# Log-softmax backward: the second y as one 64 KiB-run load, the first group's exp through PSUM, the second store in half rows

## Chip, cores, metric

One core of one Trainium2 chip. The metric is the device time of one execution in microseconds, median of several runs.

## The reference

```python
def setup_inputs():
    batch, seq_len, vocab = 8, 1024, 8192
    ...            # y = log_softmax(x), dy = randn, both (8, 1024, 8192) float32

def reference(y, dy):
    softmax_x = np.exp(y)
    sum_dy = np.sum(dy, axis=-1, keepdims=True)
    return (dy - softmax_x * sum_dy).astype(np.float32)
```

Two tensors of 268 MB are read, one is written: 805 MB in all, with little arithmetic.

## The kernel before

Rows are handled in 32 groups of 256: 128 partitions, two rows of 8192 in each. Two groups make a pair. Each has its own dy tile of 64 KiB a partition (result in place); the y tiles of both overlap in one buffer, the first shifted by SHIFT columns, so that the three buffers take 207 KiB a partition where four full tiles would take 256.

```python
SHIFT = 3840
PIECES_A = [(0, 1024), (1024, D - SHIFT), (D - SHIFT, D)]
PIECES_B = [(0, 2048), (2048, 5120), (5120, D)]
x_ts = [pool.tile([P, W], fp32, name=f"x{j}") for j in range(2)]   # W = 2 * 8192
y_t = pool.tile([P, SHIFT + W], fp32, name="y_t")
...
def compute(x, s_t, at, r, pieces):
    for b, e in pieces:
        ...
        nc.scalar.activation(y_t[:, ys], y_t[:, ys], EXP)           # exp in place
        nc.vector.scalar_tensor_tensor(out=x[:, xs], in0=y_t[:, ys],
            scalar=s_t[:, r : r + 1], in1=x[:, xs], op0=ALU.mult, op1=ALU.add)

for g in range(0, G, 2):
    load_dy(g, x_ts[0])
    load_y(g, SHIFT, 0, W)
    s_t = sums(x_ts[0])
    for r in range(R):
        compute(x_ts[0], s_t, SHIFT, r, PIECES_A)
    load_dy(g + 1, x_ts[1])
    s_t = sums(x_ts[1])
    for r in range(R):
        load_y(g + 1, 0, r * D, (r + 1) * D)                        # the second y, row by row
        compute(x_ts[1], s_t, 0, r, PIECES_B)
    for j in range(2):
        nc.sync.dma_start(out=out_v[g + j], in_=x_ts[j][:])
```

All transfers go through one queue, issued in program order by the sequencer SP. The load of the second y overwrites part of the first, so it must wait until that part has been used.

## Time and profile before

| | before |
|---|---|
| time, median of 3 runs | 1867.12 us (1866.89 to 1867.31) |
| busy share: DVE (VectorE), ACT (ScalarE) | 46%, 37% |
| busy share: the queue's 16 DMA engines | 99.8% |
| rate over the span | 432 GB/s |

The kernel is bound by its transfers. The lines that show it are in the prediction below.

### The profile page before, as it was taken

What the parts mean: (1) busy time and instruction counts of PE and PEld (TensorE: products, weight loads), DVE (VectorE), ACT (ScalarE), POOL (GpSimd) and SP (SyncE); (2) the same over time, 40 slices, a digit from 0 to 9 for tenths busy, and PEclk for the clock granted to TensorE, in tenths of its full rate; (3) what the DMA queues carried; (4) which work ended last, traced back from release to release, by engine and by line L of the source; (5) the groups of instructions that cost most, each with busy time, mean ns of one, the idle gap of its engine ahead of it and who ended that gap; (6) DMA issues with size and microseconds to landing.
All of it is one profiled execution on the core that took longest, in us unless ns stands there. A gap on an engine that the chain in (4) does not pass through costs nothing.

```text
span 1866.1 us, 843 instructions
## 1 busy us (share of the span) xinstructions
DVE 857.9 (46%) x256; ACT 689.3 (37%) x257; POOL 0.2 (0%) x4
## 2 busy tenths in 40 slices
DVE  2907429074290742807328073280732806338163
ACT  2606326063260532605326053260523605235152
POOL 0000000000000000000000000000000000000000
DMA  9999999999999999999999999999999999999998
GB/s 427 427 427 427 431 444 429 427 434 443 427 434 438 425 435 442 428 429 431 440 431 430 438 427 436 437 440 427 430 438 435 428 437 428 438 435 434 434 428 386
DMA packets 16134, 805.36 MB, mean 432 GB/s; under 512 B 1792, under 2 KB 1792, under 8 KB 1792
## 3 DMA queue, kind: packets, MB, share of 16 engines
q1 hardware_dynamic: 16128, 805.31, 99.8%
q14 instruction: 6, 0.05, 0.0%
HBM read 536.87 MB, written 268.44 MB: 432 GB/s over the span
## 4 chain that ended last, share of the span: by engine, by line
DMA 65%; DVE 14%; another core or an unknown queue 10%; ACT 9%; issue 0%; DVEq 0%; ACTq 0%; SPq 0%
DMA x<-in_dy_dram 31%; DMA out_dram<-x 30%; DVE x L74 14%; ACT x L60 6%; ACT y_t L73 3%; DMA y_t<-in_y_dram 3%; DVEq L121 0%; ACTq L121 0%; SPq L52 0%; ACTq L73 0%; ACTq L60 0%
## 5 line engine op out<-in xcount | busy, mean ns | idle before, releaser
L74 DVE SCALAR_TENSOR_TENSOR x<-y_t,s_t,x 128x1024 f32<-128x1024 f32 (+2 forms) x192 | 579.4, 3059 | 257.5 <-ACT y_t L73 257.5
L57 DVE TENSOR_REDUCE s_t<-x 128x1 f32<-128x8192 f32 x32 | 277.8, 8682 | 721.9 <-DMA x<-in_dy_dram 721.9
L73 ACT ACTIVATE y_t<-y_t 128x1024 f32<-128x1024 f32 (+2 forms) x192 | 460.1, 2466 | 280.0 <-DMA y_t<-in_y_dram 280.0
L60 ACT ACTIVATE x<-x 128x8192 f32<-128x8192 f32 x32 | 225.0, 7030 | 863.2 <-DMA x<-in_dy_dram 863.2
L60 ACT ACTIVATION_READ_ACCUMULATOR x<-x 128x1 f32 x32 | 6.0, 187 | 0.0
L61 DVE TENSOR_SCALAR s_t<-second_t 128x1 f32<-128x1 f32 x32 | 4.6, 143 | 0.0
L60 ACT ACT_TABLE_LOAD x1 | 1.3, 1283 | 0.7 <-PEq L110 0.7
L110 POOL MEMSET const-uint8-127<- 128x1 uint8 x1 | 0.1, 102 | 0.0
L110 POOL MEMSET const-bfloat16-1.0<- 128x1 bf16 x1 | 0.1, 101 | 0.0
L110 POOL MEMSET const-float32-0.0<- 128x1 f32 x1 | 0.1, 98 | 0.2 <-issue 0.2
L110 POOL MEMSET const-float32-1.0<- 128x1 f32 x1 | 0.1, 98 | 0.0
## 6 DMA issues: line engine op xcount, KB each, us to landing
y_t<-in_y_dram SPq DMA_DIRECT2D x32, 4096.0 KB, 22.1
x<-in_dy_dram SPq DMA_DIRECT2D x32, 48.4
out_dram<-x SPq DMA_DIRECT2D x32, 32.6
y_t<-in_y_dram SPq DMA_DIRECT2D x16, 57.5
```

The lines of the kernel that those rows point to most:

```text
L57: nc.vector.tensor_reduce(out=s_t[:, 0:1], in_=x[:, :D], axis=mybir.AxisListType.X, op=ALU.add, negate=True)
L60: nc.scalar.activation(x[:, D:], x[:, D:], COPY, accum_out=second_t[:])
L61: nc.vector.tensor_scalar(out=s_t[:, 1:2], in0=second_t[:], scalar1=-1.0, scalar2=None, op0=ALU.mult)
L73: nc.scalar.activation(y_t[:, ys], y_t[:, ys], EXP)
L74: nc.vector.scalar_tensor_tensor(out=x[:, xs], in0=y_t[:, ys], scalar=s_t[:, r : r + 1], in1=x[:, xs], op0=ALU.mult, op1=ALU.add,)
L110: nc = _bacc.Bacc("TRN2", target_bir_lowering=False, num_devices=1)
```

## The change

The intent: the second y comes in one load of 64 KiB runs instead of two of 32 KiB. To make its place free sooner, exp of the first group goes to PSUM, so that the load waits only until y has been read by exp and not until DVE has used the result. The second store goes row by row, so that its first half may leave while the second is computed.

```diff
-    SHIFT = 3840
+    SHIFT = 3968
-    PIECES_A = [(0, 1024), (1024, D - SHIFT), (D - SHIFT, D)]
+    PIECES_A = [(0, 1088), (1088, 2656), (2656, D - SHIFT), (D - SHIFT, 6208), (6208, D)]
+    psum = ctx.enter_context(tc.tile_pool(name="psum", bufs=2, space=bass.MemoryType.PSUM))
 ...
-            nc.scalar.activation(y_t[:, ys], y_t[:, ys], EXP)
+            if through_psum:
+                e_t = psum.tile([P, 2048], fp32, name="e_t")
+                e_ap = e_t[:, : e - b]
+            else:
+                e_ap = y_t[:, ys]
+            nc.scalar.activation(e_ap, y_t[:, ys], EXP)
 ...
-            compute(x_ts[0], s_t, SHIFT, r, PIECES_A)
+            compute(x_ts[0], s_t, SHIFT, r, PIECES_A, True)
         load_dy(g + 1, x_ts[1])
         s_t = sums(x_ts[1])
+        load_y(g + 1, 0)
+        store(g, x_ts[0], 0, W)
         for r in range(R):
-            load_y(g + 1, 0, r * D, (r + 1) * D)
-            compute(x_ts[1], s_t, 0, r, PIECES_B)
-        for j in range(2):
-            nc.sync.dma_start(out=out_v[g + j], in_=x_ts[j][:])
+            compute(x_ts[1], s_t, 0, r, PIECES_B, False)
+            store(g + 1, x_ts[1], r * D, (r + 1) * D)
```

More of the change, by code (lines that the diff above doesn't have):

```diff
@@ L64, in sums, with load_y, store, compute @@
         return s_t
-    def load_y(g, at, lo, hi):
-        nc.sync.dma_start(out=y_t[:, at + lo : at + hi], in_=y_v[g][:, lo:hi])
-    def compute(x, s_t, at, r, pieces):
+    def load_y(g, at):
+        nc.sync.dma_start(out=y_t[:, at : at + W], in_=y_v[g])
+    def store(g, x, lo, hi):
+        nc.sync.dma_start(out=out_v[g][:, lo:hi], in_=x[:, lo:hi])
+    def compute(x, s_t, at, r, pieces, through_psum):
         for b, e in pieces:
@@ L72, in compute @@
             ys = slice(at + r * D + b, at + r * D + e)
-            nc.scalar.activation(y_t[:, ys], y_t[:, ys], EXP)
+            if through_psum:
[4 more added lines that the diff above has]
+            nc.scalar.activation(e_ap, y_t[:, ys], EXP)
             nc.vector.scalar_tensor_tensor(
                 out=x[:, xs],
-                in0=y_t[:, ys],
+                in0=e_ap,
                 scalar=s_t[:, r : r + 1],
@@ L84 @@
         load_dy(g, x_ts[0])
-        load_y(g, SHIFT, 0, W)
+        load_y(g, SHIFT)
         s_t = sums(x_ts[0])
         for r in range(R):
-            compute(x_ts[0], s_t, SHIFT, r, PIECES_A)
+            compute(x_ts[0], s_t, SHIFT, r, PIECES_A, True)
         load_dy(g + 1, x_ts[1])
         s_t = sums(x_ts[1])
+        load_y(g + 1, 0)
+        store(g, x_ts[0], 0, W)
         for r in range(R):
-            load_y(g + 1, 0, r * D, (r + 1) * D)
-            compute(x_ts[1], s_t, 0, r, PIECES_B)
-        for j in range(2):
-            nc.sync.dma_start(out=out_v[g + j], in_=x_ts[j][:])
+            compute(x_ts[1], s_t, 0, r, PIECES_B, False)
+            store(g + 1, x_ts[1], r * D, (r + 1) * D)
 _INS = ['y', 'dy']
```

## The prediction

> **What bounds the kernel now.** I read the page first, then the DMA queue's own waits, then one steady stretch of the timeline, then the groups by shape. The kernel works on pairs of groups, 16 pairs in all; a pair loads dy and y twice and stores twice, six transfers of 8 MiB.
>
> From the page:
>
> ```profile
> span 1866.1 us, 843 instructions
> DVE 857.9 (46%) x256; ACT 689.3 (37%) x257; POOL 0.2 (0%) x4
> ...
> DMA  9999999999999999999999999999999999999998
> ...
> q1 hardware_dynamic: 16128, 805.31, 99.8%
> ...
> HBM read 536.87 MB, written 268.44 MB: 432 GB/s over the span
> ```
>
> The reader is to see that no compute engine is busy for half the time, while the 16 DMA engines are busy in every one of the 40 slices. So time on DVE and ACT matters only where it leaves the DMA queue empty. The waits of the DMA queue's issuing sequencer look alarming:
>
> ```profile
> SPq L67 <- DMA y_t<-in_y_dram: 615.0, 16, 39.7
> SPq L95 <- DVE x L74: 526.6, 32, 30.0
> SPq L52 <- DMA out_dram<-x: 386.4, 30, 18.5
> SPq L67 <- DVE x L74: 260.4, 32, 8.6
> ```
>
> They sum to nearly the whole span, yet the engines behind the queue are 99.8% busy: the sequencer waits with earlier transfers still in flight. What counts is the slack, from the moment a transfer is issued to the moment the queue ahead of it is drained. I read it from the timeline of the third pair, whose first y has landed at 275.7:
>
> ```profile
> 275.68 14.32 ACT L73 ACTIVATE y_t<-y_t 128x1024 f32<-128x1024 f32 x6 [12.23 <-DMA y_t<-in_y_dram]
> ...
> 283.35 9.25 SPq L67 DMA_DIRECT2D y_t<-in_y_dram  x2
> 294.96 7.03 ACT L60 ACTIVATE x<-x 128x8192 f32<-128x8192 f32 x1 [4.97 <-DMA x<-in_dy_dram]
> ...
> 304.68 7.22 ACT L73 ACTIVATE y_t<-y_t 128x2048 f32<-128x2048 f32 x3 [2.59 <-DMA y_t<-in_y_dram]
> ...
> 314.44 7.22 ACT L73 ACTIVATE y_t<-y_t 128x2048 f32<-128x2048 f32 x3 [2.55 <-DMA y_t<-in_y_dram]
> ...
> 333.87 0.34 SPq L52 DMA_DIRECT2D x<-in_dy_dram  x1
> ...
> 353.28 0.33 SPq L52 DMA_DIRECT2D x<-in_dy_dram  x1
> 372.61 8.69 DVE L57 TENSOR_REDUCE s_t<-x 128x1 f32<-128x8192 f32 x1 [46.83 <-DMA x<-in_dy_dram]
> ...
> 392.02 8.16 ACT L73 ACTIVATE y_t<-y_t 128x1024 f32<-128x1024 f32 x4 [12.23 <-DMA y_t<-in_y_dram]
> ```
>
> Each of these lines starts when a transfer has landed, so their differences are transfer times with no idle queue between: second dy 19.3 us, the two halves of the second y 9.7 + 9.8, first store 19.4, second store 19.4, next dy 19.3, next y 19.4; 116.3 us a pair. The first half of the second y was issued at 283.35, while the dy ahead of it landed at 294.96: slack 11.6 us. Sixteen such pairs make 1861 us of the 1866.
>
> The packet records in the trace give the same floor more finely. A 64 KiB packet takes 2418 ns in the median, loads and stores alike, a 32 KiB packet 1213 to 1215 ns, and a completion write 9 ns. Each engine moves 640 of the first, 256 of the second and 112 of the third: 1547.5 + 310.5 + 1.0 = 1859.1 us. The other 7 us are start, end, and some slow packets, most of them in the second half-load of y in the first few pairs.
>
> **What the Trainium skill says.** "DMA: Bandwidth & Descriptors", section Where 436 GB/s comes from, gives 435.2 GB/s as the ceiling of the ports. 805.31 MB at that rate is 1850 us (an estimate from that page): even a perfect queue gains 0.9%. The trace's 432 GB/s agrees with standing at this ceiling. "Perfetto Trace Analysis", section Optimizing Scalar/DVE Operations, has a fixed cost per instruction of about 60 ns on DVE from SBUF and 125 from PSUM, and about 93 ns on ScalarE for SBUF and 51 for PSUM. The trace of before has no PSUM operand, so it cannot confirm this; it bears on the new exps and their DVE readers. "DMA: Bandwidth & Descriptors", section Rules for kernel authors, says that DMA has no route to PSUM: so y still lands in SBUF and only exp's result moves.
>
> **The change part by part.** *The second y as one transfer of 64 KiB runs.* It replaces 16 half-load packets an engine and pair by 8 full ones: 16 x 1.213 = 19.41 against 8 x 2.418 = 19.34 us, 0.07 us a pair. *The second store as two transfers of 32 KiB runs* gives the same 0.07 us back. The number of transfers stays 7 a pair, of packets too: 640 and 256 an engine again. By the clean packets the two cancel, floor 1859.1 us. What may be won is the slow packets of the second half-load: the 32 KiB packets average 1223.6 against 1213, 256 x 0.0106 = 2.7 us an engine in all, if the 32 KiB stores do not show the same.
>
> *Exp through PSUM.* The one transfer now waits for more: it overwrites 16384 columns, of which the first y uses all from 3968 on, so row 0 and the first 4224 columns of row 1. These are exactly eight of the ten new pieces. But it waits for their exps alone, no longer for the DVE instructions that read them. I work out when the eighth exp ends. The durations are from these groups:
>
> ```profile
> L74 DVE SCALAR_TENSOR_TENSOR x<-y_t,s_t,x 128x2048 f32<-128x2048 f32 x32 | 75.2, 2351 | 34.5 <-ACT y_t L73 34.5
> L73 ACT ACTIVATE y_t<-y_t 128x2048 f32<-128x2048 f32 x32 | 61.1, 1910 | 84.4 <-DMA y_t<-in_y_dram 84.4
> L74 DVE SCALAR_TENSOR_TENSOR x<-y_t,s_t,x 128x1024 f32<-128x1024 f32 x32 | 41.0, 1281 | 188.0 <-ACT y_t L73 188.0
> L73 ACT ACTIVATE y_t<-y_t 128x1024 f32<-128x1024 f32 x32 | 33.5, 1048 | 195.6 <-DMA y_t<-in_y_dram 195.6
> ```
>
> Between the two sizes, a column costs 1.045 ns on DVE and 0.84 on ACT, with 0.21 and 0.19 us fixed. So pieces of 1088, 1568 and 1984 cost 1.35, 1.85 and 2.28 us on DVE, 1.10, 1.50 and 1.85 on ACT. There are two PSUM buffers, so exp n waits for the DVE instruction n-2; I give each hand-over 0.05 us. From the landing of y, exps end at 1.10, 2.60, 4.10, 6.40, 8.25, 9.88, 12.56, 14.06: after the third, DVE mostly sets the pace. The load is issued at 14.1, some 0.5 us more for the issue, against a queue that the second dy keeps full until 19.3. **Slack falls from 11.6 to about 4.7 us, and stays positive.** Added: 4 instructions a pair on each of ACT and DVE, 64 x 0.2 us on each over the kernel, beside transfers.
>
> The rest of a pair, from the same zero: DVE ends the first group at 21.0, so the first store is issued 17 us before the second y lands at 38.6. The second group starts there. Row 0 takes 1.9 us for the first exp and 2.35 + 2 x 3.4 us on DVE (plus small gaps): half-store issued at 50, while the first store runs until 58. Row 1 is ready at 59.2, while the first half-store runs until 67.6. The next dy waits for the first store and is issued at 59.6, the next y right after; the queue is then full until 77. The last of the waits, the dy behind both half-stores, is issued near 77.5 with 38 us queued. The queue never runs dry, so the change has nothing large to remove and nothing large to add. Sum: 1867.1 - 1.6 (half or so of the 2.7) = **1865.5 us**.
>
> **The rivals.** *A: the load comes late.* The chain to exp eight holds six DVE instructions. The 0.065 us more for PSUM on the skill's page makes 0.4 us of them. Only 0.7 us or more each would eat the slack; every microsecond beyond it costs 16 us, and 2% (37 us, 2.3 us a pair) needs about 1.1 us each. For it: slack shrinks most just here. Against it: the size needed. It would give 1870 to 1905. *B: half-row stores are slow.* For it: in the first pair the second half-load took 10.7 us, not 9.7. Were all half stores to lose 1 us a pair, 16 us: 1883. Against it: most pairs show 9.8, and stores of 64 KiB run like loads. *C: the slow half-loads vanish entirely and the start is smoother*: 1863. In all three, earlier release of y is by itself worth nothing, for it was never the wait that left the queue empty.
>
> **Range and chances.** The floor and common ends bound the good side near 1861; a mild A or B bounds the other at 1871. Faster by over 2% would mean 1830, under the 1850 of the ceiling: 0.5%. Slower by over 2% needs A in force: 2.5%. Within: 97%.
>
> **What would show it.** In the profile after: the queue's share above 99% and 432 GB/s; 16128 packets; the second y issued 14 to 15 us after the first has landed; DVE and ACT each up by some 13 us; the pair at 116 us. A dry stretch of the DMA after the second dy would prove A; stretches of half stores over 9.8 us would prove B. A span outside 1861 to 1871 makes the prediction wrong.

## The result, and the profile after

The changed kernel takes 1879.88 us in the median of 4 runs (1873.0 to 1881.9); before, 1867.21 in the same rounds. It is slower: ratio 1.0061, 95% interval 1.0034 to 1.0087. All ratios here are the mean time of one kernel's fast runs over that of the other's in the same rounds, so not quite the ratio of the medians. The time lies 9 us above the top of the predicted range. Note also its scatter: 9 us between runs, against 1 us before.

From the page of the changed kernel:

```profile
span 1876.7 us, 1000 instructions
DVE 867.2 (46%) x320; ACT 699.9 (37%) x321; POOL 0.2 (0%) x4
...
DMA  9999999999999999999999999999999999999999
...
q1 hardware_dynamic: 16128, 805.31, 99.8%
...
HBM read 536.87 MB, written 268.44 MB: 429 GB/s over the span
```

Almost everything is as forecast: DVE is up by 9 us and ACT by 11, there are 16128 packets, the queue is busy 99.8% of the span, no slice is dry. (DVE and ACT were to rise by some 13.) Only the rate fell, from 432 to 429 GB/s. So **the loss is not idle time that the page can show; some packets take longer.** The sequencer's waits (who waits for whom: us in total, times, longest):

```profile
SPq L72 <- DVE x L84: 718.1, 48, 30.8
SPq L69 <- DMA y_t<-in_y_dram: 615.7, 16, 40.1
SPq L54 <- DMA out_dram<-x: 247.1, 17, 17.1
SPq L69 <- ACT e_t L83: 219.2, 16, 13.7
```

The last line is the new wait: the second y waits for exps, 13.7 us from the landing of the first y. That was worked out as 14.1.

Now two pairs of the changed kernel from its timeline, the third first. Each line gives the start, the length and the instruction, in brackets the idle time before it. As in the prediction, an ACT line that waited for DMA starts when its transfer has landed, and an SPq line when the transfer is issued:

```profile
275.74 3.98 ACT L83 ACTIVATE e_t<-y_t 128x1088 f32<-128x1088 f32 x3 [12.61 <-DMA y_t<-in_y_dram]
...
289.41 0.33 SPq L69 DMA_DIRECT2D y_t<-in_y_dram  x1
...
295.03 7.03 ACT L62 ACTIVATE x<-x 128x8192 f32<-128x8192 f32 x1 [1.54 <-DMA x<-in_dy_dram]
...
314.39 14.32 ACT L83 ACTIVATE y_t<-y_t 128x2048 f32<-128x2048 f32 x6 [12.23 <-DMA y_t<-in_y_dram]
```

and the ninth:

```profile
975.29 3.98 ACT L83 ACTIVATE e_t<-y_t 128x1088 f32<-128x1088 f32 x3 [12.21 <-DMA y_t<-in_y_dram]
...
988.97 0.33 SPq L69 DMA_DIRECT2D y_t<-in_y_dram  x1
...
994.60 7.03 ACT L62 ACTIVATE x<-x 128x8192 f32<-128x8192 f32 x1 [1.55 <-DMA x<-in_dy_dram]
...
1015.54 14.32 ACT L83 ACTIVATE y_t<-y_t 128x2048 f32<-128x2048 f32 x6 [13.82 <-DMA y_t<-in_y_dram]
```

The load of the second y is issued 13.7 us after the first has landed in both, and the second dy lands 19.3 us after it in both. But the second y follows the dy by 19.36 us in the third pair and by 20.94 in the ninth. Windows of 2 us over the end of that load, in the ninth pair (columns: window, length, busy time of DVE, ACT and POOL, clock, DMA share, GB/s), show where:

```profile
1006.00:1008.00 2.00, 0.00 (x0) 0.00 (x0) 0.00 (x0) 1.00 1.21 459
1008.00:1010.00 2.00, 0.00 (x0) 0.00 (x0) 0.00 (x0) 1.00 1.29 360
1010.00:1012.00 2.00, 0.00 (x0) 0.00 (x0) 0.00 (x0) 1.00 0.67 262
1012.00:1014.00 2.00, 0.00 (x0) 0.00 (x0) 0.00 (x0) 1.00 0.91 393
```

A window books a packet to its start, so single values swing. But these four average 368 GB/s, with DVE and ACT both idle: nothing they do at that moment can be the reason.

**The packet records** say the rest. On each of the 16 engines a packet's record begins 3 to 4 ns before the end of the one before, so the records can be strung into 16 chains. Where two engines tie, the completion writes decide: each transfer ends with 16 of them, one for each engine, and their semaphore tells which transfer it was. So each packet can be named by its transfer. I call *excess* the time over the usual 2418 ns (64 KiB) or 1213 ns (32 KiB), averaged over the 16 engines. It is 4.2 us in the whole kernel before, and 14.9 us after; the difference, 10.7, is the 10.6 by which the spans differ. Of the 14.9, 13.9 lie in the second y, 10.9 of these in the last of its eight packets. (Some expectations below have 13, from a first stringing that ties had misled.) The 32 KiB stores have none (0.03).

The excess is not spread evenly. I call *lead* the time from the issue of the second y to the moment at which the *foremost* engine gets to its first packet of it:

| pair of the changed kernel | 1 | 2 | 3 | 5 | 7 | 8 | 9 | 10 | 12 | 14 | 16 |
|---|---|---|---|---|---|---|---|---|---|---|---|
| lead, us | 4.6 | 4.2 | 3.8 | 3.5 | 2.6 | 1.5 | 1.8 | 1.2 | 1.5 | 1.0 | 1.5 |
| excess of the second y, us | 0.99 | 0.01 | 0.11 | 0.15 | 0.08 | 1.40 | 1.50 | 1.52 | 1.52 | 1.50 | 1.52 |

The issue comes equally early in every pair. The lead shrinks because the foremost engine runs ahead of the last: their distance at the start of this load grows from 0.7 us in the first pair to 3.6 in the eighth, and stays at 3.4 to 4.4 after that. The first pair is a case of its own (below).

The same records show some idle time after all. In no run does a packet of the second y start sooner than 0.95 us after the load is issued. In the pairs from the eighth on, one to six engines end the second dy before their first packet of the load starts, and wait, some of them until 3 us or more after the issue: 0.9 us per engine over the kernel, against none in the second y of before. The total does not show it, since in the profiled run the engines end the kernel closer together by as much.

### The profile page after: what moved, and what is told of

The parts are those of the page before. It is cut to its first block, busy times and chain, and to the rows that moved or that the text cites. A ratio compares the mean times of both kernels' runs of the same rounds, so it can differ in the third digit from the quotient of the medians.

```text
span 1876.7 us, 1000 instructions
## 1 busy us (share of the span) xinstructions
DVE 867.2 (46%) x320; ACT 699.9 (37%) x321; POOL 0.2 (0%) x4
## 3 DMA queue, kind: packets, MB, share of 16 engines
q1 hardware_dynamic: 16128, 805.31, 99.8%
## 4 chain that ended last, share of the span: by engine, by line
DMA 54%; DVE 18%; ACT 16%; another core or an unknown queue 10%; issue 1%; SPq 0%; DVEq 0%; ACTq 0%
DMA x<-in_dy_dram 30%; DMA y_t<-in_y_dram 24%; DVE x L84 18%; ACT e_t L83 6%; ACT x L62 6%; ACT y_t L83 4%; SPq L72 0%; DVEq L131 0%; ACTq L131 0%; SPq L54 0%; ACTq L83 0%; ACTq L62 0%
## 5 line engine op out<-in xcount | busy, mean ns | idle before, releaser
L84 DVE SCALAR_TENSOR_TENSOR x<-e_t,s_t,x 128x1984 f32<-128x1984 f32 (+2 forms) x160 | 300.5, 1919 | 199.5 <-ACT e_t L83 194.3
L84 DVE SCALAR_TENSOR_TENSOR x<-y_t,s_t,x 128x3072 f32<-128x3072 f32 (+1 forms) x96 | 288.3, 3057 | 201.0 <-ACT y_t L83 201.0
L83 ACT ACTIVATE e_t<-y_t 128x1984 f32<-128x1984 f32 (+2 forms) x160 | 241.5, 1535 | 239.5 <-DMA y_t<-in_y_dram 197.0
L83 ACT ACTIVATE y_t<-y_t 128x3072 f32<-128x3072 f32 (+1 forms) x96 | 229.2, 2465 | 208.2 <-DMA y_t<-in_y_dram 208.2
```

The source lines that it names most:

```text
L83: nc.scalar.activation(e_ap, y_t[:, ys], EXP)
L84: nc.vector.scalar_tensor_tensor(out=x[:, xs], in0=e_ap, scalar=s_t[:, r : r + 1], in1=x[:, xs], op0=ALU.mult, op1=ALU.add,)
```

## The experiments

All eleven runs passed the comparison with the reference. Four (e3, e4, e5, e11) compute something wrong; that they pass shows only that the comparison doesn't see the correction to dy, which is small. The bookkeeping of all, from the profiled runs; *idle* is time without a packet in flight, per engine, from the first packet of the kernel to the last, the end included, where some engines finish before others:

| run | median us | ratio to before | span | excess | idle | excess in the second y |
|---|---|---|---|---|---|---|
| before | 1867.21 | | 1866.1 | 4.2 | 3.6 | 2.7 |
| changed | 1879.88 | 1.0061 | 1876.7 | 14.9 | 3.6 | 13.9 |
| e1 one load only | 1960.02 | 1.0498 | 1957.5 | 42.1 | 57.6 | 27.0 |
| e2 halves back | 1867.85 | 1.0004 | 1866.1 | 3.4 | 3.7 | 2.2 |
| e3 other rows | 1876.87 | 1.0048 | 1873.3 | 12.5 | 2.5 | 11.5 |
| e4 no compute | 1866.57 | 0.9996 | 1864.9 | 3.5 | 3.1 | 2.5 |
| e5 load early | 1867.93 | 1.0004 | 1866.7 | 3.9 | 4.5 | 2.6 |
| e6 one exp later | 1901.19 | 1.0184 | 1897.7 | 29.0 | 10.4 | 28.0 |
| e7 exp in place | 1891.84 | 1.0127 | 1890.4 | 26.3 | 5.8 | 25.2 |
| e8 store whole | 1936.00 | 1.0370 | 1933.8 | 31.1 | 45.0 | 15.6 |
| e10 late halves | 1903.26 | 1.0197 | 1900.4 | 29.0 | 12.3 | 28.2 |
| e11 late, bare | 1897.66 | 1.0160 | 1896.0 | 29.8 | 7.9 | 29.0 |

In each row the excess and idle time over those of before add up to the difference of the spans within 1 us. (e9 moves more bytes and stands apart.)

### One load only

```diff
 (before)
+        load_y(g + 1, 0, 0, W)
         for r in range(R):
-            load_y(g + 1, 0, r * D, (r + 1) * D)
             compute(x_ts[1], s_t, 0, r, PIECES_B)
```

> Before, with the one edit that the second y of a pair comes as one transfer of 64 KiB runs; exp stays in place, stores stay whole. Theory T1 (the long runs of the second y are what is slow: the packet records of the changed kernel show 14.8 us of excess over 2418 ns per engine, 13 of it in that load, mostly its last packet): 1872 to 1882 us and the same excess in that load. Rival T2 (the loss comes with the half-row stores or with exp through PSUM): 1865 to 1868 us, excess under 4 us. Rival T3 (the load comes too late and the queue runs dry): idle engine time between packets would appear, which the changed kernel does not show (0.2 us a kernel), so no more than 1 us of it.

Measured: 1960.02 us, more than any theory foresaw. Two things came together. The load waits for DVE and has a lead of 1.7 to 1.9 us in every pair: 27 us of excess. And the whole second store is ready only when the first has drained, so the queue runs dry for some 3 us a pair, and the last packet of the store after it takes 0.8 us more. So the PSUM and half-row parts of the change are what makes one load bearable; this run alone doesn't tell which of them counts.

### Halves back

```diff
 (changed kernel)
-        load_y(g + 1, 0)
+        for r in range(R):
+            nc.sync.dma_start(out=y_t[:, r*D:(r+1)*D], in_=y_v[g+1][:, r*D:(r+1)*D])
```

> The changed kernel, with the second y again as two transfers of 32 KiB runs; exp through PSUM and half-row stores kept. T1: back to 1864 to 1868 us, excess in the second y under 4 us. T2: stays at 1873 to 1882 us.

Measured: 1867.85 us, as before. PSUM, new pieces and half-row stores cost nothing; the loss came with the single load. But the halves also let the first of them go out earlier, so length and moment aren't told apart yet.

### Other rows

```diff
-        load_y(g + 1, 0)
+        nc.sync.dma_start(out=y_t[:, 0:W], in_=y_v[g])
```

> The changed kernel, with the second y read from the first group's rows (wrong result on purpose), so from HBM addresses 8 MiB lower, all else the same. If where in HBM the rows lie makes them slow: excess in that load falls to under 3 us and the time to 1864 to 1868 us. If the place in the sequence (last load before a store) does it: the same 13 us of excess, 1873 to 1882 us.

Measured: 1876.87 us, 11.5 us of excess in the second y. The rows' place in HBM is not the cause. The pairs of this run repeat the table above: leads of 2.9 us and more (pairs 2 to 7) go with 0.06 to 0.15 us of excess, leads of 1.0 to 1.7 (pairs 8 to 14) with 0.97 to 1.84. In the last two pairs the lead recovers to 2.6 and 2.4, and the excess falls to 0.04 and 0.21: so it isn't the late part of the kernel that is slow.

### No compute

```diff
-        s_t = sums(...)         # both
-            compute(...)        # both
```

> The changed kernel's transfers alone, all work of ACT and DVE taken out (wrong result on purpose: it stores dy). If what ACT and DVE do, or when transfers are issued because of them, slows the load: no excess, 1863 to 1866 us. If it is the sequence of transfers itself: the same 13 us of excess in the second y, 1873 to 1882 us.

Measured: 1866.57 us, excess 2.5 us in the second y, at leads of 14.9 to 18.5 us. The sequence of transfers with its 64 KiB runs is as good as the old one, and hardly better: **the medians differ by 0.6 us in 1867**, and the interval of the ratio, 0.9982 to 1.0011, includes no difference at all. What ACT and DVE do, or when transfers are issued because of it, is the cause.

### Load early

The exps of the second row read columns of the y tile that the second y doesn't overwrite, so that its load needs to wait for five exps only:

```diff
             ys = slice(at + r * D + b, at + r * D + e)
+            if through_psum and r == 1:
+                ys = slice(W, W + e - b)
```

> The changed kernel, with the exps of the first group's second row reading the part of the y tile beyond the second y (wrong result on purpose), so that the one load of the second y waits for five exps instead of eight and is issued some 6 us earlier; 64 KiB runs, PSUM, half-row stores and all counts stay. Theory L (lead: a load issued less than one 64 KiB packet, 2.4 us, before the foremost DMA engine has drained its queue costs 1 to 2 us at the last packet of that run of loads; in the changed kernel the lead falls from 4.6 us in the first pair to under 2 from the eighth on, and the excess starts there): lead 9 to 11 us, excess of the second y under 3 us, time 1864 to 1868. Rival R (the long load beside the work of ACT and DVE is slow in itself): excess stays near 13 us, 1873 to 1882.

Measured: 1867.93 us. One pair of its timeline beside that of the changed kernel above:

```profile
974.48 3.98 ACT L85 ACTIVATE e_t<-y_t 128x1088 f32<-128x1088 f32 x3 [12.22 <-DMA y_t<-in_y_dram]
...
982.49 0.33 SPq L69 DMA_DIRECT2D y_t<-in_y_dram  x1
...
993.79 7.03 ACT L62 ACTIVATE x<-x 128x8192 f32<-128x8192 f32 x1 [1.55 <-DMA x<-in_dy_dram]
...
1013.13 14.32 ACT L85 ACTIVATE y_t<-y_t 128x2048 f32<-128x2048 f32 x6 [12.22 <-DMA y_t<-in_y_dram]
```

The load goes out 8.0 us after the first y instead of 13.7, and takes 19.34 us after the dy instead of 20.94. The work of ACT and DVE is the same, instruction for instruction; only the moment differs. Leads are 5.5 to 10.3 us. The excess of 2.6 is that of the kernel before. The lead shrinks here too, by some 5 us over the kernel, but from a safe start.

### One exp later

```diff
-    SHIFT = 3968
+    SHIFT = 1984      # pieces unchanged: the load now waits for the ninth exp
```

> The changed kernel with a shift of 1984 columns instead of 3968 and the same piece sizes (right result): the load of the second y waits for nine exps, so about 2.3 us later, all else the same. L: lead near 2 us in every pair, so 1.4 to 2 us of excess in each of 16 pairs instead of nine: 1888 to 1900 us. R, or the sheer length of runs: unchanged, 1873 to 1882. A queue that runs dry as well would show idle time between packets.

Measured: 1901.19 us, 1 us over the expected range. The same pair in this run:

```profile
988.28 3.98 ACT L83 ACTIVATE e_t<-y_t 128x1088 f32<-128x1088 f32 x3 [12.21 <-DMA y_t<-in_y_dram]
...
1004.30 0.33 SPq L69 DMA_DIRECT2D y_t<-in_y_dram  x1
...
1007.57 7.03 ACT L62 ACTIVATE x<-x 128x8192 f32<-128x8192 f32 x1 [1.54 <-DMA x<-in_dy_dram]
...
1029.81 14.32 ACT L83 ACTIVATE y_t<-y_t 128x2048 f32<-128x2048 f32 x6 [15.11 <-DMA y_t<-in_y_dram]
```

Issued at 16.0 us, landed 22.24 us after the dy. From the second pair on every lead is 0.9 to 1.6 us and every excess 1.5 to 2.0; idle time adds 7 us. (In eleven of these pairs the lead is 0.95 to 0.98: the foremost engine had run dry and waited for the load, four times since before its issue.) The result is right, so this is a mere choice of buffer shift that costs 21 us over the changed kernel.

The first packets of the second y in this run show the threshold engine by engine: those that begin 1.0 to 1.2 us after the issue take 0.76 us longer than usual in the median, those that begin at 2.0 to 2.2 us nothing. And an engine need not have waited for it: in pair 14 none did, at a lead of 1.2 us, and the excess is 1.71 us.

### Exp in place

```diff
-            compute(x_ts[0], s_t, SHIFT, r, PIECES_A, True)
+            compute(x_ts[0], s_t, SHIFT, r, PIECES_A, False)
```

> The changed kernel with exp back in place (PSUM undone): the load of the second y waits for eight DVE instructions instead of eight exps, about 2 to 3 us later. L: like the run before this, 1888 to 1900 us, excess in every pair. If PSUM itself slows something: faster than the changed kernel, under 1873.

Measured: 1891.84 us. Without PSUM the load waits for DVE and is later again. So the PSUM part does what it was meant to do, 12 us' worth, but not enough. This run narrows the threshold: pair 2 has a lead of 2.2 us and 0.15 us of excess, pair 3 a lead of 1.8 and 0.94.

### Store whole

```diff
-            store(g + 1, x_ts[1], r * D, (r + 1) * D)    # in the row loop
+        store(g + 1, x_ts[1], 0, W)                      # after it
```

> The changed kernel with the second store whole (half-row stores undone). The store is ready about 2.5 us after the first store has drained, so the queue runs dry in each pair: 16 x (2.9 + 0.8) us as in the run with the one load alone, 1925 to 1936 us. L adds: the dry queue lines the engines up again in every pair, so the lead of the second y stays at 4.5 us and its excess falls under 3 us. R: 13 us of excess there too, 1938 to 1946.

Measured: 1936.00 us; by the page, the queue's engines are busy for less of the span:

```profile
q1 hardware_dynamic: 13824, 805.31, 97.7%
```

Without half-row stores the queue truly runs dry: 41 us more of idle time than before. The time fits. But one expectation fell: the second y has 0.64 to 1.28 us of excess in *every* pair, though its lead is 3.8 us or more. So a late load isn't the only way to a slow last packet. The same 0.9 to 1.2 stands in the first pair of nearly every run, before included, whatever the lead. Both come after a start from a dry queue, with all engines within 0.8 us of each other (1.2 and 1.3 in two pairs of this run). Being close together is not enough by itself: the second pair of e2 has a distance of 0.5 us and an excess of 0.11. What exactly is needed stays open; in the changed kernel it touches only the first pair, as it does before.

### A load behind

```diff
 (e6, with)
         load_y(g + 1, 0)
+        nc.sync.dma_start(out=y_t[:, W : W + SHIFT], in_=y_v[g + 1][:, 0:SHIFT])
```

> The late kernel (shift 1984, load of the second y after nine exps, 28 us of excess in that load) with one more, unneeded load of 1 MiB queued between the second y and the store (right result; 2.4 us of transfer a pair, so some 39 us more). If the price of the late load is paid by its own last packet: the excess stays there. If it is paid where loads give way to a store: the excess moves to the last packets of the extra load. Time 1935 to 1945 either way; if a load behind it lets the late load off altogether, about 1910.

Measured: 1938.37 us (2 runs). In e6, 18.4 of the 28.0 us lie in the second y's last packet. Here that packet has 0.6, and the extra load some 16, spread over its short packets, though it is issued 19 us or more before the foremost engine gets to it. The first packet of the second y, which had 8.4 us in e6, has about 9 here. So the price has two parts: a smaller one where the late load begins, and a larger one wherever the run of loads gives way to a store.

### Late halves

```diff
 (e6, with)
-        load_y(g + 1, 0)
+        for r in (1, 0):                # two loads of 32 KiB runs, both issued late
+            nc.sync.dma_start(out=y_t[:, r*D:(r+1)*D], in_=y_v[g+1][:, r*D:(r+1)*D])
```

> The late kernel again, but the second y as two loads of 32 KiB runs, both issued at the late moment, the upper row first. If the lead that is needed is one packet of the size in hand (1.2 us for 32 KiB): most pairs are spared as long as the lead stays near 2 us, 1867 to 1880. If it is a fixed time of over 2 us: excess in every pair as with 64 KiB, 1888 to 1905.

Measured: 1903.26 us, no better than with 64 KiB. Even the second pair, with a lead of 1.6 us, more than one 32 KiB packet, pays 0.4 in its first half-load and 0.9 in its second. So the needed lead is not one packet of the size in hand; a time of about 2 us fits, and the run length is acquitted.

### Late, bare

```diff
 (e4, with)
+        at = [r*D + b for r in range(R) for b, e in PIECES_A if r == 0 or e <= D - SHIFT]
+        for b in at + at[2:5]:          # 11 exps that read y and hold its place
+            e_t = psum.tile([P, 2048], fp32, name="e_t")
+            nc.scalar.activation(e_t[:, :1568], y_t[:, SHIFT+b : SHIFT+b+1568], EXP)
```

> The transfers alone once more (wrong result on purpose), with nothing on the engines but a chain of 11 exps of 1568 columns into PSUM, which holds the load of the second y back to some 16.5 us after the first y has landed. L: the lateness alone brings the loss back, 1.5 to 2 us a pair, 1888 to 1903 us, against 1866.6 for the same transfers without the chain. If the work of DVE, or the moment of the store, is what matters: 1866 to 1870.

Measured: 1897.66 us. The sequencer's waits name what was put in:

```profile
SPq L69 <- ACT e_t L99: 248.7, 16, 15.8
```

No DVE work, no sums; nothing but the hold-up of one transfer, and 31 us are lost over the same transfers without it.

## Why the prediction was wrong

- **Right: the kernel is bound by its transfers, and there is nothing large to win.** The bare transfers take 1866.57 us. (The floor of 1859.1 adds the packet records end to end; as they overlap by 3 to 4 ns, about 3.4 us of it are counted twice.)
- **Right: the instruction times and the chain.** The eighth exp was to end 14.06 us after the landing; the load was issued at 13.7. Pieces of 1088, 1568 and 1984 columns were to take 1.35, 1.85 and 2.28 us on DVE and took 1.346, 1.847 and 2.279. Rival A's "0.7 us or more each" never came about.
- **Right: 32 KiB stores are as good as loads**, even better: of the 2.7 us of slow half packets of before, 0.03 are left in the half stores. But the hoped-for gain of 1.6 us was not there: with 64 KiB runs and every load early, e4 and e5 still have 2.5 and 2.6 us in the second y.
- **Wrong: "Slack falls from 11.6 to about 4.7 us, and stays positive", and from it "The queue never runs dry, so the change has nothing large to remove and nothing large to add".** Two terms of this were mis-sized. First, I took the time at which the queue drains from landings, which show the last engine. The foremost engine gets there earlier, by 0.7 us in the first pair and by 3.6 in the eighth, so 4.7 us of slack were 4.6 at the start and 1.0 to 1.8 from the eighth pair on. Second, I took zero as the threshold. The runs put it near 2 us: a lead of 1.8 or less cost 0.78 to 2.1 us in the pairs looked at (e6, e7, e11 and the changed kernel), and 2.2 to 5 cost 0.01 to 0.21 (e3, e7 and the changed kernel; with more lead 0.4 at most), first pairs and e8 aside; in e1, 1.7 to 1.9 cost 1.4 to 2.0. With nine of sixteen pairs at 0.78 to 1.52 us, 11 us were lost, against a forecast gain of 1.6.
- **Wrong: the sign by which rival A would show.** I wrote that "A dry stretch of the DMA after the second dy would prove A". Rival A, the load that comes late, is what happened, and the time is inside its 1870 to 1905. But the idle time in total did not rise (3.6 us in both); only 0.9 us of it moved to the beginning of the late loads. The loss sits in packets that take longer, which a busy share counts as busy. I gave rival A too small a chance because I measured it against a dry queue.

Shown: the lateness of one load is the cause (e5 takes it away and the loss goes; e6, e7 and e11 add to it and the loss about doubles or more; e10 does so with short runs); most of the price is paid at the end of the run of loads (e9). Not shown is why the changed kernel scatters by 9 us. That the lead crosses the threshold at another pair in each run would do it, and in e3 it even recovers; but e7, whose lead is short from the third pair on, scatters as widely (1886.35 to 1895.44). Not shown either: the mechanism. The page "DMA: Bandwidth & Descriptors" of the Trainium skill, section Latency and other measured facts, gives "0.2 µs avg, 2 µs at high load" for an access to HBM. A read side that must be that far ahead of the write side would fit a threshold of 2 us and a bill at the end of the loads; no run here observes it. Nor did I find why the engines drift apart.

No version of these beats the kernel before by anything that the runs can tell: e5 and e2 are level with it, and so is e4, without any work on the engines.

## What to carry to other kernels

In a kernel at the rate of its transfers, keep every load queued well before the *foremost* DMA engine needs it: here over 2 us, plus some 3 to 5 us for the engines' drift. Slack read from landing times is that of the last engine and flatters. And a busy share of 99.8% does not prove that nothing is lost; compare the rate, or the times of single packets, in the stretches around each hand-over.

## What the Trainium skill lacked or had wrong

- "DMA: Bandwidth & Descriptors" has no figure for how far ahead of a busy queue a transfer must be issued. Here: at 1.8 us of lead or less, 0.8 to 2.1 us of longer packets a transfer, most of it in the last packets before a store; in the changed kernel the engines idled for only 0.9 us with it.
- The same page, section Why a DMA increments its semaphore by 16 and not by 1, says that the 16 engines finish independently, but not that they drift apart: from 0.7 us in the first pair to 3.4 to 4.4 from the eighth on in the changed kernel, and from 0.7 to 5.3 in e5, with most 64 KiB packets at 2418 ns.
- "Perfetto Trace Analysis", section Optimizing Scalar/DVE Operations, has DVE pay about 65 ns more for PSUM than for SBUF, as engine-busy time. In the profile's rows the difference is nil, with one of the two inputs in PSUM: 1568 columns took 1847 ns in the changed kernel and 1847 in e7, which has the same pieces in place. ScalarE took 1472 ns into PSUM against 1493 in e7, and 1825 against 1840 for 1984 columns: 15 to 21 less, where the page's figures differ by 42.
